# Placing weight tiles at chosen byte distances, modulo 256, from the other matmul operand

## The chip, the cores and the metric

One core of one Trainium2 chip runs the whole program. The metric is the device time of one execution in microseconds (us), as the median of several runs. A hardware profile of one execution stands beside it.

## The reference

One decoder layer on 256 tokens of width 2048, in float32: a half-step SwiGLU, a mixer of two branches, and a second half-step SwiGLU, each between two RMS norms.

```python
def swiglu(h, w_gate, w_up, w_down):
    return (jax.nn.silu(h @ w_gate) * (h @ w_up)) @ w_down
...
    h = rmsnorm(x, ffn1_norm_pre[l])
    x = x + MACARON_SCALE * rmsnorm(swiglu(h, ...), ffn1_norm_post[l])
    h = rmsnorm(x, mix_norm_pre[l])
    y = token_mixer(h, ...)   # sigmoid(gate_a)*attention + sigmoid(gate_b)*hgrn2, times w_out
    x = x + rmsnorm(y, mix_norm_post[l])
    h = rmsnorm(x, ffn2_norm_pre[l])
    x = x + MACARON_SCALE * rmsnorm(swiglu(h, ...), ffn2_norm_post[l])
```

Widths: the SwiGLU steps go from 2048 to 5632 and back; the mixer projects 2048 to 13376 columns, has 16 attention heads over latents of width 512, and 16 heads of a gated linear recurrence (hgrn2). Nearly all of the arithmetic is the products of 256 tokens with weight matrices.

## The kernel before

**Split operands.** Float32 precision is had from float32r matmuls by splitting each operand in two parts: `hi`, the value rounded to float32r, and `lo`, the remainder. A product is hi·hi + hi·lo + lo·hi. `load_w` brings 128x1024 weights (512 KB) by DMA into `raw`, ScalarE casts `raw` to `hi` (L101), VectorE subtracts to get `lo` (L102). The tiles `whi` and `wlo` have four buffers each of 1024 float32 a partition. Activations lie in tiles of the form [128, 2, K tiles, 256], whose second axis is hi and lo: `h` (the tiles h1, after1 and h2 in the program), `at`, `oa`, `ob`, `mg`, `cqT`, `ckvT`.

**Two kinds of product.** A TensorE matmul loads a stationary operand of 128 columns (LDWEIGHTS, the engine row PEld) and streams a moving operand past it. While one matmul streams, the stationary operand of the next is loaded.

- *Column products*, `gemm_t`: the weights are stationary and the activations move, so the outputs come out with the product's columns on the partitions. For each K tile and each half of 256 columns there is a pair: `lo` weights against 256 moving columns (L122, the activations' hi), and `hi` weights against 512 (L123, the activations' hi and lo side by side). For the first K tile the pair stands the other way round (L119, L120). One load of 1024 weights feeds eight such pairs. The gate and up products, all gates of the mixer, the q/f projections of hgrn2, both output projections of the branches and the small products of attention are of this kind: 4224 pairs.
- *Row products*, `gemm_n`: the activations are stationary and the weights move, 512 columns at a time, three matmuls for each K tile and half of the tokens (`_tok`: L138 hi·hi, L139 lo·hi, L140 hi·lo). One load feeds twelve matmuls. The down products, `w_out`, the first 512 columns of gate and up, the latents, the values and gates of hgrn2 and the rope part of the queries are of this kind; `w_v` too, with 256 columns at a time. At the end of a stage (`late`, `own`) some loads are held for a second pass; those lie in buffers `wpair` of the stage's pool, hi and lo one behind the other.

**Addresses.** A pool's tiles lie one behind the other in a partition. In the program before, all buffers of `whi` and `wlo` start at byte 96 modulo 256; `h`, `at`, `oa`, `ob`, `mg` and `wpair` at 224; `cqT` and `ckvT` at 160. Every K tile and half within a tile is a whole number of 256 bytes further on. So the distance, by which this document means *the start of the moving operand less the start of the stationary operand that is loaded meanwhile, modulo 256 bytes*, is one number for a whole product:

| product | moving, stationary | distance before |
|---|---|---|
| row, `whi`/`wlo` against `h`, `at`, `mg` | 96, 224 | 128 |
| row, `wpair` against `h`, `at`, `mg` | 224, 224 | 0 |
| row, `whi`/`wlo` against `cqT` (`q_rope`) | 96, 160 | 192 |
| row, 256 wide, against `ckvT` (`w_v`) | 96, 160 | 192 |
| column, `h`, `oa`, `ob` over `whi`/`wlo` | 224, 96 | 128 |
| column, `cqT`, `ckvT` over `whi`/`wlo` | 160, 96 | 64 |

**Order.** The program order of TensorE is that of the source: products follow each other without a break where their loads are early enough. All weight loads go out on one queue (SP), with four `raw` buffers ahead.

**Other tiles that the change touches.** `sg` in `ffn` holds a gate product of 256 columns from its end to the end of the up product after it (about 22 us), with two buffers; `z0`, `z1` are the tiles of the down product's results, unused until then. `rope_tables` has five small temporaries (`ang`, `turns`, three parts); `pT` holds transposed attention weights later on.

Of the kernel before, what the change touches and what calls it, by code (L numbers as in the profile page):

```python
# [9 lines left out]
F32 = mybir.dt.float32  # L10
# [33 lines left out]

WARM = 10

TWO_PI = 2.0 * np.pi
MAGIC = 1.5 * 2.0 ** 23

# [13 lines left out]
class Ops:  # L63


    def __init__(self, ctx, tc, a):
        self.tc, self.nc, self.a = tc, tc.nc, a
        self.const = ctx.enter_context(tc.tile_pool(name="const", bufs=1))
        self.wp = ctx.enter_context(tc.tile_pool(name="wp", bufs=1))
        self.small = ctx.enter_context(tc.tile_pool(name="small", bufs=3))  # L70
        self.hp = ctx.enter_context(tc.tile_pool(name="hp", bufs=1))
        self.mm = ctx.enter_context(tc.tile_pool(name="mm", bufs=2, space=PSUM))
        self.tp = ctx.enter_context(tc.tile_pool(name="tp", bufs=2, space=PSUM))
        self.sp = ctx.enter_context(tc.tile_pool(name="sp", bufs=2, space=PSUM))
        self.dram = ctx.enter_context(tc.tile_pool(name="dram", bufs=1, space=DRAM))
        self.slots = KF // 4
        self.mhalf = self.const.tile([P, 8], F32, name="mhalf")
        self.nc.vector.memset(self.mhalf, -0.5)
        self.ident = self.const.tile([P, P], F32, name="ident")


    def load_w(self, src, pool=None, pieces=1):
        nc = self.nc
        raw = self.wp.tile([P, 1024], F32, name="raw", bufs=4)
        if pieces > 1:
            hi = self.wp.tile([P, 1024], F32R, name="whi", bufs=4)
            lo = self.wp.tile([P, 1024], F32R, name="wlo", bufs=4)
            n = 1024 // pieces
            for i in range(pieces):
                c = slice(i * n, (i + 1) * n)  # L90
                nc.sync.dma_start(out=raw[:, c], in_=src[:, c])
                self.split(hi[:, c], lo[:, c], raw[:, c])
            return hi, lo
        nc.sync.dma_start(out=raw, in_=src)
        if pool is None:
            hi = self.wp.tile([P, 1024], F32R, name="whi", bufs=4)
            lo = self.wp.tile([P, 1024], F32R, name="wlo", bufs=4)
        else:
            both = pool.tile([P, 2, 1024], F32R, name="wpair", tag="s8", bufs=self.slots)
            hi, lo = both[:, 0], both[:, 1]  # L100
        nc.scalar.copy(out=hi, in_=raw)  # L101
        nc.vector.tensor_tensor(out=lo, in0=raw, in1=hi.bitcast(F32), op=ALU.subtract)  # L102
        return hi, lo

    def gemm_t(self, w, act, kt, tick=None):

        nc = self.nc
        ps = self.mm.tile([P, 2, 512], F32, name="mm")  # L110
        for g in range(kt // 4):
            hi, lo = self.load_w(w[g])
            for i in range(4):
                k = g * 4 + i
                for j in range(2):
                    c = slice(i * 256 + j * P, i * 256 + (j + 1) * P)
                    both = act(k)
                    if k == 0:
                        nc.tensor.matmul(ps[:, j], hi[:, c], both, start=True, stop=False)  # L119
                        nc.tensor.matmul(ps[:, j, 0:T], lo[:, c], both[:, 0], start=False, stop=False)  # L120
                    else:
                        nc.tensor.matmul(ps[:, j, 0:T], lo[:, c], both[:, 0], start=False, stop=False)  # L122
                        nc.tensor.matmul(ps[:, j], hi[:, c], both, start=False, stop=k == kt - 1)  # L123
            if tick:
                tick()
        return ps
# [12 lines left out]
        nc.tensor.matmul(o, both[:, 0, r], lo[:, c], start=False, stop=False)  # L139
        nc.tensor.matmul(o, both[:, 1, r], hi[:, c], start=False, stop=k == kt - 1)  # L140

    def gemm_n(self, w, act, kt, n=512, late=0, pool=None, own=0, hooks=(), tick=None):

        kg = 1024 // n
        banks = self.mm.tile([P, 2, 512], F32, name="mm")
        ps = [banks[:, 0], self.mm.tile([P, 2, 512], F32, name="mm")[:, 1] if late else banks[:, 1]]  # L150
        held = []
        hooks = list(hooks)

        def call(at):
            while hooks and hooks[0][0] <= at:
                hooks.pop(0)[1](ps)

        for g in range(kt // kg):
            hold = g * kg >= kt - late
            hi, lo = self.load_w(w[g], pool if hold and g * kg >= kt - late + own * kg else None)  # L160
            call(g * kg / kt - 1)
            for i in range(kg):
                k = g * kg + i
                self._tok(ps, hi, lo, act, k, kt, i, n, 0)
                if hold:
                    held.append((hi, lo, k, i))
                else:
                    self._tok(ps, hi, lo, act, k, kt, i, n, 1)
            if tick:
                tick()  # L170
        for m, (hi, lo, k, i) in enumerate(held):
            call(m / len(held))
            self._tok(ps, hi, lo, act, k, kt, i, n, 1)
        call(1)
        return ps if late else banks
# [128 lines left out]
def layer_kernel(ctx, tc, a, out):  # L304
# [75 lines left out]
    def ffn(n, act, fp, x_src, x_dst, nxt, hooks=(), fac=None, first=None):  # L380
        at = [fp.tile([P, 2, 4, T], F32R, name="at", tag="s8", bufs=ops.slots) for _ in range(KF // 4)]
        wg, wu = a[f"ffn{n}_w_gate"], a[f"ffn{n}_w_up"]


        if first:
            rows, first = first
        else:
            pg = ops.gemm_n(a[f"ffn{n}_w_gate0"], act, KD, late=KD, pool=fp, own=4, hooks=hooks)
            pu = ops.gemm_n(a[f"ffn{n}_w_up0"], act, KD, late=KD, pool=fp, own=4)
            rows = ops.rows(fac, fp.tile([P, T], F32, name="rows", tag="z0"))  # L390
            for tt in range(NT):
                sg = ops.small.tile([P, 512], F32, name="xn", bufs=2)
                S.activation(out=sg, in_=pg[tt], func=AF.Silu, scale=fac[:, tt, 2:3])
                V.scalar_tensor_tensor(out=sg, in0=pu[tt], scalar=fac[:, tt, 2:3], in1=sg, op0=ALU.mult, op1=ALU.mult)
                ops.transposed(sg, at[0], 0, tt)

        for c in range((FF - FF_N) // 256):
            pg = ops.gemm_t(wg[c], act, KD)
            if first and c == 0:
                for tt in range(NT):  # L400
                    ops.transposed(first[tt], at[0], 0, tt)
            sg = fp.tile([P, 2, T], F32, name="sg", bufs=2)
            ops.total(sg, pg, rows)
            S.activation(out=sg, in_=sg, func=AF.Silu)
            pu = ops.gemm_t(wu[c], act, KD)
            su = ops.small.tile([P, 2, T], F32, name="m", bufs=2)
            ops.total(su, pu, rows)
            V.tensor_tensor(out=sg, in0=sg, in1=su, op=ALU.mult)
            k = FF_N // P + 2 * c
            t, i = at[k // 4], k % 4  # L410
            ops.split(t[:, 0, i:i + 2], t[:, 1, i:i + 2], sg)
        new = operand(f"after{n}") if nxt else (None, None)
        fac = ops.factors(f"fac_after{n}") if nxt else None
        hooks = ops.closing(a[f"ffn{n}_w_down"], lambda k: at[k // 4][:, :, k % 4, :], KF, 16, 3, fp,
                    f"ffn{n}_norm_post", True, x_src, x_dst, (nxt, new[0], fac) if nxt else None)
        return *new, fac, hooks
# [69 lines left out]
def rope_tables(ops, pool):  # L486
# [7 lines left out]
    freq = pool.tile([P, HALF], F32, name="freq")  # L494
    nc.sync.dma_start(out=freq, in_=a["inv_freq"].broadcast_to([P, HALF]))
    n = NT * HALF
    ang = pool.tile([P, n], F32, name="ang")
    for tt in range(NT):
        V.tensor_scalar(out=ang[:, tt * HALF:(tt + 1) * HALF], in0=freq, scalar1=pos[:, tt:tt + 1],
                        scalar2=None, op0=ALU.mult)  # L500
# [2 lines left out]
        V.tensor_scalar(out=dst, in0=src, scalar1=MAGIC * step, scalar2=MAGIC * step, op0=ALU.add, op1=ALU.subtract)  # L503


    turns = pool.tile([P, n], F32, name="turns")
    parts = [pool.tile([P, n], F32, name=f"part{i}") for i in range(3)]
    for use in ((2, 1, 0), (0,)):
        V.tensor_scalar(out=turns, in0=ang, scalar1=1.0 / TWO_PI, scalar2=None, op0=ALU.mult)
        for i in use:  # L510
# [17 lines left out]
def mla(ops, mp, c_q, hm, h, fac, rows, oa, gate):  # L528
# [35 lines left out]

    hi, lo = ops.load_w(a["w_krope"][0])
    ps = ops.mm.tile([P, 2, 512], F32, name="mm")
    for k in range(KD):
        c = slice(k * ROPE, (k + 1) * ROPE)  # L570
# [23 lines left out]
    qrT = mp.tile([P, NH // 2, T], F32, name="qrT")  # L594

    def q_rope(c):
        ps = ops.gemm_n(a["w_q_rope"][c], cq, KL)
        for tt in range(NT):
            qr = small.tile([P, 8, ROPE], F32, name="xn", bufs=2)
            rope(qr, ps[:, tt].rearrange("p (a b) -> p a b", b=ROPE), tt, 8)  # L600
# [6 lines left out]
    def heads_in(pair, step):  # L607
        qn = mp.tile([P, 2, T], F32, name="qn", bufs=3)
        ops.total(qn, ops.gemm_t(a["w_q_nope"][pair], cq, KL))
        step()  # L610
        kn = mp.tile([P, 2, T], F32, name="kn", bufs=3)
        ops.total(kn, ops.gemm_t(a["w_k_nope"][pair], ckv, KL))
        step()
        ps = ops.gemm_n(a["w_v"][pair], ckv, KL, n=256)
        v = mp.tile([P, NT, 256], F32, name="v", bufs=3)
        S.copy(out=v, in_=ps[:, :, 0:256])
        return pair, qn, kn, v
# [389 lines left out]
```

## Time and profile before

| | |
|---|---|
| median of 3 runs | 2532.18 us (2531.83 to 2532.49) |
| the profiled execution's own time | 2530.82 us |
| its span, first to last instruction | 2528.9 us |
| mean granted TensorE clock | 0.999 |
| PE busy | 2512.3 us (99%) |
| PEld busy | 2144.2 us (85%) |
| VectorE, ScalarE, GpSimd busy | 1546.1 (61%), 1211.2 (48%), 82.1 us (3%) |
| moved by DMA | 482.12 MB, mean 191 GB/s |

Matmuls are pipelined, and a row's duration runs from a matmul's start to the modelled end of its results, which lies after the start of the next. The cost of one matmul in a dense stretch is therefore the step from its start to the next one's start, which the timeline shows to 10 ns; over many matmuls the mean step is known to a fraction of a nanosecond.

### The profile page before, as it was taken

To read this page: it belongs to the slowest core of one execution; us is meant where nothing else is said; L and a number is where in the kernel's file an instruction comes from. 1 tells how busy PE (TensorE), PEld (TensorE's weight loads), DVE (VectorE), ACT (ScalarE), POOL (GpSimd) and SP (SyncE) were. 2 spreads that over 40 slices of the span, in tenths; PEclk is the share of its full clock that TensorE was granted. 3 is DMA by queue.
4 is the path that set the end of the run, shared out by engine and by line. 5 is a ranking of instruction groups with operands and counts; after the bars stand their busy time and mean duration, and the time that the engine had idled before them with its cause. 6 is when DMAs were issued, how large, how long until landed. Compare 5 with 4: busy or idle time off the path is not lost.

```text
span 2528.9 us, 33917 instructions
## 1 busy us (share of the span) xinstructions
PE 2512.3 (99%) x13306; PEld 2144.2 (85%) x13306; DVE 1546.1 (61%) x1845; ACT 1211.2 (48%) x1605; POOL 82.1 (3%) x108
## 2 busy tenths in 40 slices
PE   9999999999999999999999999999999999999998
PEld 7888888888877898888888888888788888888887
DVE  5656656544466666558778876655655666654444
ACT  6444444444354566444555555445444444444433
POOL 0000000000000100000000001110000000000000
PEclk9999999999999999999999999999999999999999
DMA  8555555556575444555555555567655555555655
GB/s 299 185 188 187 185 190 189 186 191 201 194 282 181 162 135 149 189 184 183 175 166 168 167 166 175 191 223 235 221 188 188 186 188 187 185 190 191 196 196 183
DMA packets 137680, 482.12 MB, mean 191 GB/s; under 512 B 15920, under 2 KB 16432, under 8 KB 136752
## 3 DMA queue, kind: packets, MB, share of 16 engines
q1 hardware_dynamic: 137520, 479.96, 57.5%
q8 instruction: 104, 1.70, 0.3%
q14 instruction: 56, 0.46, 0.1%
HBM read 473.61 MB, written 6.29 MB: 190 GB/s over the span
## 4 chain that ended last, share of the span: by engine, by line
PE 97%; DVE 1%; DMA 1%; POOL 1%; issue 0%; ACT 0%; SPq 0%; DVEq 0%; POOLq 0%; ACTq 0%
PE mm L123 36%; PE mm L122 19%; PE mm L139 12%; PE mm L140 12%; PE mm L138 12%; PE mm L119 3%; PE mm L120 1%; PE sp L841 1%; PE sp L629 0%; PE sp L628 0%; PE sp L829 0%; PE tp L660 0%; DVE x L283 0%; PE tp L237 0%; DMA raw<-in_w_cq 0%
## 5 line engine op out<-in xcount | busy, mean ns | idle before, releaser
L102 DVE TENSOR_TENSOR wlo<-raw,whi 128x1024 fp32r<-128x1024 f32 x832 | 1031.5, 1242 | 701.9 <-ACT whi L101 695.1
L101 ACT CAST whi<-raw 128x1024 fp32r<-128x1024 f32 x832 | 872.7, 1050 | 866.1 <-PE mm L123 455.6
L123 PE MATMUL mm<-h,whi 128*128 128x512 f32 x2400 | 846.0, 393 | 0.0
L122 PE MATMUL mm<-h,wlo 128*128 128x256 f32 x2400 | 678.1, 283 | 0.0
L123 PEld LDWEIGHTS mm<-h,whi 128*128 128x128 f32 x2400 | 450.7, 188 | 100.7
L122 PEld LDWEIGHTS mm<-h,wlo 128*128 128x128 f32 x2400 | 451.2, 188 | 3.9
L123 PE MATMUL mm<-after,whi 128*128 128x512 f32 x960 | 339.5, 394 | 0.0
L122 PE MATMUL mm<-after,wlo 128*128 128x256 f32 x960 | 273.0, 284 | 0.0
L138 PE MATMUL mm<-whi,at 128*128 128x512 f32 x664 | 262.0, 395 | 0.0
L139 PE MATMUL mm<-wlo,at 128*128 128x512 f32 x664 | 262.0, 395 | 0.0
L140 PE MATMUL mm<-whi,at 128*128 128x512 f32 x664 | 261.7, 395 | 0.0
L123 PEld LDWEIGHTS mm<-after,whi 128*128 128x128 f32 x960 | 180.4, 188 | 39.3
L122 PEld LDWEIGHTS mm<-after,wlo 128*128 128x128 f32 x960 | 180.5, 188 | 1.5
L139 PEld LDWEIGHTS mm<-wlo,at 128*128 128x128 f32 x664 | 125.0, 188 | 29.4
L140 PEld LDWEIGHTS mm<-whi,at 128*128 128x128 f32 x664 | 125.1, 188 | 29.2
L138 PEld LDWEIGHTS mm<-whi,at 128*128 128x128 f32 x664 | 125.1, 188 | 29.1
L138 PE MATMUL mm<-whi,after 128*128 128x512 f32 x304 | 122.5, 403 | 0.4 <-ACT after L178 0.4
L140 PE MATMUL mm<-whi,after 128*128 128x512 f32 x304 | 120.1, 395 | 0.0
L139 PE MATMUL mm<-wlo,after 128*128 128x512 f32 x304 | 120.0, 395 | 0.0
L123 PE MATMUL mm<-oa,whi 128*128 128x512 f32 x240 | 84.6, 393 | 0.0
L123 PE MATMUL mm<-ob,whi 128*128 128x512 f32 x240 | 84.6, 393 | 0.0
L130 ACT COPY m<-mm 128x512 f32<-128x512 f32 x56 | 32.9, 588 | 97.1 <-PE mm L123 97.1
(306 smaller groups left out, 2819.4 us busy)
## 6 DMA issues: line engine op xcount, KB each, us to landing
raw<-in_ffn_w_down SPq DMA_DIRECT2D x176, 512.0 KB, 4.3
raw<-in_ffn_w_gate SPq DMA_DIRECT2D x175, 512.0 KB, 4.3
raw<-in_ffn_w_up SPq DMA_DIRECT2D x175, 512.0 KB, 4.3
raw<-in_w_ga SPq DMA_DIRECT2D x32, 512.0 KB, 3.4
raw<-in_mla_w_o SPq DMA_DIRECT2D x32, 512.0 KB, 3.8
raw<-in_w_hq SPq DMA_DIRECT2D x32, 512.0 KB, 3.5
raw<-in_w_hf SPq DMA_DIRECT2D x32, 512.0 KB, 3.4
raw<-in_w_hi SPq DMA_DIRECT2D x32, 512.0 KB, 3.5
```

The source lines that it names most:

```text
L101: nc.scalar.copy(out=hi, in_=raw)
L102: nc.vector.tensor_tensor(out=lo, in0=raw, in1=hi.bitcast(F32), op=ALU.subtract)
L119: nc.tensor.matmul(ps[:, j], hi[:, c], both, start=True, stop=False)
L120: nc.tensor.matmul(ps[:, j, 0:T], lo[:, c], both[:, 0], start=False, stop=False)
L122: nc.tensor.matmul(ps[:, j, 0:T], lo[:, c], both[:, 0], start=False, stop=False)
L123: nc.tensor.matmul(ps[:, j], hi[:, c], both, start=False, stop=k == kt - 1)
L130: self.nc.scalar.copy(out=out, in_=ps[:, :, T:512])
L138: nc.tensor.matmul(o, both[:, 0, r], hi[:, c], start=k == 0, stop=False)
L139: nc.tensor.matmul(o, both[:, 0, r], lo[:, c], start=False, stop=False)
L140: nc.tensor.matmul(o, both[:, 1, r], hi[:, c], start=False, stop=k == kt - 1)
L841: nc.tensor.matmul(ps[:, 0, j], B[:, j], A[:, j], start=True, stop=True)
```

## The change

The buffers of `whi` and `wlo` become 64 float32 (256 bytes) wider, and a part starts `place` float32 into its buffer. In row products the place is 32 (128 bytes), so `whi` and `wlo` start at 224 and the distance to `h`, `at`, `mg` is 0; 16 for `q_rope`, distance 0 to `cqT`; 0 for `w_v`, which keeps 192. In column products it goes round: with every load, `hi` moves by 8 float32 (32 bytes) through eight places, and with every eighth load `lo` does, so that 64 loads go through all 64 combinations. The small product with `w_krope` has place 0, as before. `wpair` is not touched. To make room (the wider buffers take 2048 bytes a partition), `sg` moves into the tag of `z1`, with one buffer in place of two, and the temporaries of `rope_tables` into a buffer of `pT`. The tiles that are added or taken away are whole numbers of 256 bytes, so no other tile's start changes modulo 256.

```diff
+SAME = 32
...
+    def part(self, name, place):
+
+        return self.wp.tile([P, 1024 + 64], F32R, name=name, bufs=4)[:, place:place + 1024]
+
-    def load_w(self, src, pool=None, pieces=1):
+    def load_w(self, src, pool=None, pieces=1, places=(SAME, SAME)):
...
-            hi = self.wp.tile([P, 1024], F32R, name="whi", bufs=4)
-            lo = self.wp.tile([P, 1024], F32R, name="wlo", bufs=4)
+            hi, lo = self.part("whi", places[0]), self.part("wlo", places[1])
...
+    def round(self):
+
+        i = self.count
+        self.count += 1
+        return i % 8 * 8, i // 8 % 8 * 8
+
     def gemm_t(self, w, act, kt, tick=None):
...
-            hi, lo = self.load_w(w[g])
+            hi, lo = self.load_w(w[g], places=self.round())
...
-    def gemm_n(self, w, act, kt, n=512, late=0, pool=None, own=0, hooks=(), tick=None):
+    def gemm_n(self, w, act, kt, n=512, late=0, pool=None, own=0, hooks=(), tick=None, place=SAME):
...
-            hi, lo = self.load_w(w[g], pool if hold and g * kg >= kt - late + own * kg else None)
+            hi, lo = self.load_w(w[g], pool if hold and g * kg >= kt - late + own * kg else None,
+                                 places=(place, place))
...
-            sg = fp.tile([P, 2, T], F32, name="sg", bufs=2)
+            sg = fp.tile([P, 2, T], F32, name="sg", tag="z1")
...
-    ang = pool.tile([P, n], F32, name="ang")
+    tmp = pool.tile([P, 3 * P], F32, name="angles", tag="pT", bufs=2)
+    ang, turns, *parts = (tmp[:, i * n:(i + 1) * n] for i in range(5))
...
-    turns = pool.tile([P, n], F32, name="turns")
-    parts = [pool.tile([P, n], F32, name=f"part{i}") for i in range(3)]
...
-    hi, lo = ops.load_w(a["w_krope"][0])
+    hi, lo = ops.load_w(a["w_krope"][0], places=(0, 0))
...
-        ps = ops.gemm_n(a["w_q_rope"][c], cq, KL)
+        ps = ops.gemm_n(a["w_q_rope"][c], cq, KL, place=SAME - 16)
...
-        ps = ops.gemm_n(a["w_v"][pair], ckv, KL, n=256)
+        ps = ops.gemm_n(a["w_v"][pair], ckv, KL, n=256, place=0)
```

More of the change, by code (lines that the diff above doesn't have):

```diff
@@ L76, in __init__ @@
         self.slots = KF // 4
+        self.count = 0
         self.mhalf = self.const.tile([P, 8], F32, name="mhalf")
@@ L95, in load_w @@
         if pool is None:
-            hi = self.wp.tile([P, 1024], F32R, name="whi", bufs=4)
-            lo = self.wp.tile([P, 1024], F32R, name="wlo", bufs=4)
+            hi, lo = self.part("whi", places[0]), self.part("wlo", places[1])
         else:
```

## The prediction, made before the change was run

> **What bounds the kernel now.** First the page's busy times, then its chain of waits: TensorE is busy nearly all the time, and the chain that ends last runs through it.
>
> ```profile
> PE 2512.3 (99%) x13306; PEld 2144.2 (85%) x13306; DVE 1546.1 (61%) x1845; ACT 1211.2 (48%) x1605; POOL 82.1 (3%) x108
> ```
>
> ```profile
> PE 97%; DVE 1%; DMA 1%; POOL 1%; issue 0%; ACT 0%; SPq 0%; DVEq 0%; POOLq 0%; ACTq 0%
> ```
>
> So time goes only if the steps from one matmul to the next shrink, and a step saved in a dense stretch is saved in the span. Next the groups by line, in which "x" is a count and the last number before the second bar a mean duration in ns:
>
> ```profile
> L102 DVE TENSOR_TENSOR wlo<-raw,whi 128x1024 fp32r<-128x1024 f32 x832 | 1031.5, 1242 | 701.9 <-ACT whi L101 695.1
> L101 ACT CAST whi<-raw 128x1024 fp32r<-128x1024 f32 x832 | 872.7, 1050 | 866.1 <-PE mm L123 455.6 <-PE mm L140 368.9 <-issue 16.8
> L123 PE MATMUL mm<-h,whi 128*128 128x512 f32 x2400 | 846.0, 393 | 0.0
> L122 PE MATMUL mm<-h,wlo 128*128 128x256 f32 x2400 | 678.1, 283 | 0.0
> ```
>
> L122 and L123 are the column products. For the row products the view of one line, L139, keeps the operands apart, with shortest, median and longest duration in ns:
>
> ```profile
> L139 PE MATMUL mm<-wlo,at x664: 387/393/404, 502.5 to 2513.5; 128*128 128x512 f32 x166
> L139 PE MATMUL mm<-wlo,after x304: 387/393/477, 750.0 to 1498.1; 128*128 128x512 f32 x152
> L139 PE MATMUL mm<-wlo,mg x108: 387/393/404, 1685.7 to 1767.1; 128*128 128x512 f32 x108
> L139 PE MATMUL mm<-wlo,h x96: 387/394/500, 6.4 to 1818.7; 128*128 128x512 f32 x96
> L139 PE MATMUL mm<-wlo,ckvT x64: 276/276/281, 834.1 to 975.3; 128*128 128x256 f32 x64
> L139 PE MATMUL mm<-wpair,at x40: 387/389/397, 729.8 to 2520.3; 128*128 128x512 f32 x40
> L139 PE MATMUL mm<-wpair,h x32: 389/389/505, 1788.0 to 1824.1; 128*128 128x512 f32 x32
> L139 PE MATMUL mm<-wpair,mg x20: 389/389/397, 1756.8 to 1776.4; 128*128 128x512 f32 x20
> L139 PE MATMUL mm<-wpair,after x16: 387/389/499, 755.5 to 775.2; 128*128 128x512 f32 x16
> L139 PE MATMUL mm<-wlo,cqT x16: 393/394/478, 820.9 to 853.1; 128*128 128x512 f32 x16
> ```
>
> The reader is to see that the median goes with the distance, whatever the operand: 393 or 394 at 128 (`wlo` against `at`, `after`, `mg`, `h`), 394 at 192 (`cqT`), 389 at 0 (all four `wpair` rows). At 128 there are 664 + 304 + 108 + 96 = 1172 on this line, and as many on L138 and L140, which run beside it: 3516 matmuls.
>
> Last the timeline, whose first column is each matmul's start. At the start of the second SwiGLU, `wpair` and `whi`/`wlo` take turns against the same `h`, each for 24 matmuls:
>
> ```profile
> 1808.09 0.39 PE L138 MATMUL mm<-wpair,h 128*128 128x512 f32 x1
> ...
> 1813.55 0.40 PE L138 MATMUL mm<-whi,h 128*128 128x512 f32 x1
> ...
> 1819.14 0.39 PE L138 MATMUL mm<-wpair,h 128*128 128x512 f32 x1
> ```
>
> At distance 0, 24 steps take 5.46 us, or 227.5 ns each; at 128, right behind, 5.59 us, or 232.9. Longer stretches, in the last down product, give the settled steps:
>
> ```profile
> 2470.02 0.40 PE L138 MATMUL mm<-whi,at 128*128 128x512 f32 x1
> ...
> 2512.78 0.39 PE L139 MATMUL mm<-wlo,at 128*128 128x512 f32 x1
> ...
> 2516.22 0.39 PE L139 MATMUL mm<-wpair,at 128*128 128x512 f32 x1
> ...
> 2520.30 0.39 PE L139 MATMUL mm<-wpair,at 128*128 128x512 f32 x1
> ```
>
> At 128, 184 steps in 42.76 us are 232.4 ns each; at 0, 18 steps in 4.08 us are 226.7. So a median duration of 389 goes with a step of 226.7, and durations stand some 162 ns above steps: 394 at 192 is a step of about 232, and 276, for `w_v` with 256 columns at 192, one of about 114.
>
> **The row products: a price that the trace shows.** 3516 matmuls go from 128 to 0. Settled, each saves 232.4 − 226.7 = 5.7 ns; in the runs of 24, 5.4. That is 3516 × 5.7 ns = 20.0 us, or 19.0. About 200 of them stand in the first stage, beside the loads of both forms of x; should that stage wait for its loads anyway, 1.1 us of it is not had. `q_rope`, from 192 to 0, has 48 matmuls at some 6 ns, 0.3 us; `w_v` stays. I take 20 us, between 18 and 21.
>
> **The column products: a price that must be bounded.** These are 4224 pairs, and going round puts them at distances that the trace mostly doesn't have. What it has:
>
> ```profile
> 859.14 0.40 PE L119 MATMUL mm<-ckvT,whi 128*128 128x512 f32 x1
> ...
> 859.50 0.28 PE L122 MATMUL mm<-ckvT,wlo 128*128 128x256 f32 x1
> ...
> 861.61 0.28 PE L138 MATMUL mm<-whi,ckvT 128*128 128x256 f32 x1
> ...
> 1961.66 0.28 PE L122 MATMUL mm<-h,wlo 128*128 128x256 f32 x1
> ...
> 1987.63 0.28 PE L122 MATMUL mm<-h,wlo 128*128 128x256 f32 x1
> ```
>
> With both parts at distance 128, 74 pairs take 25.97 us: 350.9 ns each. With both at 64, six pairs from 859.50 to 861.61 take 2.11 us, 351.7 ns. The pair from 859.14 to 859.50 is a dear one without a wait: 360 ns. The cheapest pair that rows allow to be put together is a 512-wide step as in the row products at 0 and a 256-wide one as in `w_v`: 226.7 + 114 = 340.7 ns. So the bounds are 4224 × (340.7 − 350.9) = −43 us and 4224 × (360 − 350.9) = +38 us.
>
> Between them I go by an average, since going round visits every distance equally often. Less 162, the groups' 283 and 393 are steps of 121 and 231, which make 352 against the pair's measured 350.9; I put them at 120.4 and 230.5. For the 512-wide step the row products give 226.7 at 0, 232.4 at 128 and 232 at 192, mean 230.4: no change. For the 256-wide one there is 120.4 at 128, about 121 at 64 (351.7 − 230.8), and 114 at 192: mean 118.5, or 1.9 ns less. If the quarter that no row shows, 0, is as good for 256 columns as it is for 512, the mean is 117.3, 3.1 ns less. I take 2.8, nearer to that, since 0 was the best of all distances in rows: 4224 × 2.8 ns = 12 us saved. That the distances of `hi` and `lo` act one by one, and that odd multiples of 32 bytes lie between their neighbours, is assumed; no row shows either.
>
> **The rest costs nothing, and why.** No instruction is added or removed. Casts and subtractions write at other places; should that be slower, its cover is large. Per load VectorE works 1.24 us and ScalarE 1.05 (L102, L101), while TensorE takes 8 × 351 ns = 2.81 us (columns) or 12 × 232 ns = 2.79 us (rows), and the casts wait for TensorE to free a buffer (their releasers), so the weights stand ahead; without that cover 1 ns on each of 832 casts would be 0.8 us. The one buffer of `sg` makes ScalarE's copy at the end of a gate product wait until the `sg` before has been read, and weight casts are queued behind that copy:
>
> ```profile
> L130 ACT COPY sg<-mm x40: 586/586/586, 63.5 to 2264.5; 128x512 f32<-128x512 f32 x40
> L404 ACT ACTIVATE sg<-sg x40: 632/633/639, 66.7 to 2266.5; 128x512 f32<-128x512 f32 x40
> L178 ACT CAST at<-sg x40: 621/622/628, 79.4 to 2279.5; 128x512 fp32r<-128x512 f32 x40
> ```
>
> The `sg` copied at 63.5 is cast last at 79.4 and subtracted right behind, by 81. The next copy is due 64 pairs × 351 ns = 22.5 us after the first, at 86. Some 5 us are left over, so nothing waits. `z1` is first written in the down product, and the temporaries of `rope_tables` are done with before attention writes `pT`. The weights are asked for 1.3% faster, which the cover above bears too.
>
> **Sum.** −20 − 12 = −32 us. The profiled execution took 2530.82 us, 1.9 more than its span and 1.4 less than the median of 2532.18; the median should come to 2500.
>
> A rule to set beside the rows: the Trainium skill, TensorE: Matmul & The Clock Gate, "Back-to-back issue gap", gives N/2.4 + 2.5 ns a matmul, 215.8 for 512 columns and 109.2 for 256. If placing took every step there, the estimate from that page is a saving of some 58 us in rows and 110 in columns; no stretch read above is that fast (226.7 and 114), so the trace does not bear it out.
>
> **Rivals.**
> *The columns pay back what the rows give (slower).* Going round breaks settled patterns: each load has a new distance of `hi`, every eighth a new one of `lo`, and a pair in disorder costs up to the 360 ns seen. It decides from 20 us / 4224 = 4.7 ns a pair, a mean of 355.6; with all pairs at 360 the sum is +38 − 20 = +18 us, 2550. For it: the 360 ns pair stands right behind a change of operand, and 512-wide steps are dear at both 128 and 192. Against: the six pairs that follow it are back at 351.7.
> *The columns lose a little,* 0 to 15 us: 2512 to 2527, most likely 2517.
> *All column stalls go:* pairs at 340.7, 43 us, 2469. Every distance would have to be as good as the best; the medians of 393 and 394 at two quarters speak against it.
> *The change does nothing:* `wpair` is faster for another reason, such as less splitting beside it in the held pass: 2532. Against: the runs of 24 follow each other in one gate product, and the step changes with each.
> The Trainium skill speaks for this rival: SBUF — State Buffer, "Who interferes with whom", has independent read ports for the moving operand and LDWEIGHTS, and says that "PE and ACT never wait on anyone". By that rule the sum is 0; the trace disagrees, with 227.5 against 232.9 ns at two distances.
>
> **How the numbers follow.** Changes within 0.2% (5 us) can't be told from none here. Chances: the forecast, with columns saving up to 40 us, 0.64; columns losing up to 15, 0.18; all stalls gone, 0.04; columns taking back all or more, 0.08; distance without effect, 0.06. Faster is the first three, 0.86; same is the last, 0.06; slower 0.08. The range leaves out the two cases at the top and the fastest one: from 2474 (rows 20, columns 38) to 2526 (rows 20 less 14).
>
> **What would show it.** Right: the last down product at 226 to 228 ns a step throughout; L139's medians at 389 for `at`, `after`, `mg`, `h` and `cqT` alike, with `wpair` and `w_v` as before; L122's mean falling from 283 towards 280, L123's staying near 393, each with more spread than before. Wrong: row steps still at 232 (distance is not the cause, or more address bits count), column pairs above 355 ns in the mean, or TensorE waiting for `whi` where it did not.

## The result, and the profile after

The changed kernel takes 2506.66 us (median of 4, 2506.02 to 2506.98) where the kernel before took 2532.01 beside it: a ratio of 0.9902 (95% interval 0.989 to 0.9914), or 25.3 us less. The forecast was 2500, 32 us less. Its profiled execution took 2506.64 us with a span of 2504.7. The page's busy times, and the columns' two costliest groups (L133 and L134 are L122 and L123 of before):

```profile
PE 2486.5 (99%) x13306; PEld 2136.1 (85%) x13306; DVE 1544.9 (62%) x1845; ACT 1210.7 (48%) x1605; POOL 82.2 (3%) x108
```

```profile
L134 PE MATMUL mm<-h,whi 128*128 128x512 f32 x2400 | 842.2, 394 | 0.0
L133 PE MATMUL mm<-h,wlo 128*128 128x256 f32 x2400 | 672.0, 280 | 0.0
```

The reader is to see the mean duration go from 283 down to 280 ns for the 256-wide matmul, and from 393 up to 394 for the 512-wide one. The view of L150 (L139 before) shows the row products, with shortest, median and longest duration:

```profile
L150 PE MATMUL mm<-wlo,at x664: 388/389/389, 500.0 to 2489.3; 128*128 128x512 f32 x166
L150 PE MATMUL mm<-wlo,after x304: 387/389/478, 741.8 to 1484.8; 128*128 128x512 f32 x152
L150 PE MATMUL mm<-wlo,mg x108: 389/389/397, 1671.6 to 1751.2; 128*128 128x512 f32 x108
L150 PE MATMUL mm<-wlo,h x96: 387/389/501, 6.8 to 1802.3; 128*128 128x512 f32 x96
L150 PE MATMUL mm<-wlo,ckvT x64: 276/280/284, 825.3 to 966.5; 128*128 128x256 f32 x64
...
L150 PE MATMUL mm<-wlo,cqT x16: 389/393/475, 812.0 to 844.1; 128*128 128x512 f32 x16
```

393 or 394 became 389 for `at`, `after`, `mg` and `h`, now at distance 0; `cqT`, at 0 too, shows 393. Against `at` the spread is gone: 388 to 389 over 664 matmuls, where before it was 387 to 404. The last down product's timeline agrees:

```profile
2446.00 0.39 PE L151 MATMUL mm<-whi,at 128*128 128x512 f32 x1
...
2488.84 0.39 PE L151 MATMUL mm<-whi,at 128*128 128x512 f32 x1
```

189 steps in 42.84 us are 226.7 ns. For the columns the best gauge is a whole stage: the gate and up products of the second SwiGLU are 40 products behind each other, and the view of the line that opens each product gives the first and the last start. Before (L119), then after (L130):

```profile
L119 PE MATMUL mm<-h,whi x80: 393/397/476, 1826.1 to 2264.6; 128*128 128x512 f32 x80
```

```profile
L130 PE MATMUL mm<-h,whi x80: 387/395/481, 1809.7 to 2246.3; 128*128 128x512 f32 x80
```

Between the two starts lie 39 products of 32 pairs and one pair, 1249 pairs: 438.5 us or 351.1 ns a pair before, 436.6 us or 349.6 after. Summed over all steps in the two traces, each from one matmul's start to the next one's, row products went from 934.4 to 916.1 us (−18.3), column products, `w_krope` among them, from 1498.4 to 1492.0 (−6.4), all else by +0.5: together the 24.2 us by which the span is shorter.

### The profile page after: what moved, and what is told of

Read it like the earlier page. It is cut to its first block, busy times and chain, and to the rows that moved or that the text cites. A ratio compares the mean times of both kernels' runs of the same rounds, so it can differ in the third digit from the quotient of the medians.

```text
span 2504.7 us, 33918 instructions
## 1 busy us (share of the span) xinstructions
PE 2486.5 (99%) x13306; PEld 2136.1 (85%) x13306; DVE 1544.9 (62%) x1845; ACT 1210.7 (48%) x1605; POOL 82.2 (3%) x108
## 4 chain that ended last, share of the span: by engine, by line
PE 97%; DVE 1%; POOL 1%; DMA 1%; issue 1%; ACT 0%; SPq 0%; DVEq 0%; POOLq 0%; ACTq 0%
PE mm L134 36%; PE mm L133 18%; PE mm L151 12%; PE mm L150 11%; PE mm L149 11%; PE mm L130 3%; PE mm L131 1%; PE sp L852 1%; PE sp L640 0%; PE sp L639 0%; DVE x L295 0%; PE sp L840 0%; PE tp L671 0%; DVE xn L263 0%; DVE wlo L107 0%
## 5 line engine op out<-in xcount | busy, mean ns | idle before, releaser
L134 PE MATMUL mm<-h,whi 128*128 128x512 f32 x2400 | 842.2, 394 | 0.0
L133 PE MATMUL mm<-h,wlo 128*128 128x256 f32 x2400 | 672.0, 280 | 0.0
L134 PEld LDWEIGHTS mm<-h,whi 128*128 128x128 f32 x2400 | 450.9, 188 | 101.1
L133 PEld LDWEIGHTS mm<-h,wlo 128*128 128x128 f32 x2400 | 451.2, 188 | 3.5
L134 PE MATMUL mm<-after,whi 128*128 128x512 f32 x960 | 337.8, 394 | 0.0
L133 PE MATMUL mm<-after,wlo 128*128 128x256 f32 x960 | 270.6, 282 | 0.0
L149 PE MATMUL mm<-whi,at 128*128 128x512 f32 x664 | 258.3, 389 | 0.0
L150 PE MATMUL mm<-wlo,at 128*128 128x512 f32 x664 | 258.3, 389 | 0.0
L151 PE MATMUL mm<-whi,at 128*128 128x512 f32 x664 | 258.0, 389 | 0.0
L134 PEld LDWEIGHTS mm<-after,whi 128*128 128x128 f32 x960 | 180.4, 188 | 39.3
L133 PEld LDWEIGHTS mm<-after,wlo 128*128 128x128 f32 x960 | 180.6, 188 | 1.5
L150 PEld LDWEIGHTS mm<-wlo,at 128*128 128x128 f32 x664 | 124.6, 188 | 26.0
L150 PE MATMUL mm<-wlo,after 128*128 128x512 f32 x304 | 118.5, 390 | 0.0
L134 PE MATMUL mm<-ob,whi 128*128 128x512 f32 x240 | 84.3, 394 | 0.0
L134 PE MATMUL mm<-oa,whi 128*128 128x512 f32 x240 | 84.1, 393 | 0.0
```

The lines of the kernel that those rows point to most:

```text
L149: nc.tensor.matmul(o, both[:, 0, r], hi[:, c], start=k == 0, stop=False)
```

## The experiments

Each run is named by its label. The theory at first: a matmul's step is set by the distance, rows and columns add up, and going round gives the columns a mean over distances. Against it stand that settled patterns matter and not distances, and that the weights' own place does it.

**One part alone.** `rows_only` keeps the columns at place 0, `round_only` the rows.

```diff
 rows_only
-            hi, lo = self.load_w(w[g], places=self.round())
+            hi, lo = self.load_w(w[g], places=(0, 0))
 round_only
-SAME = 32
+SAME = 0
...
+        ps = ops.gemm_n(a["w_q_rope"][c], cq, KL, place=0)
```

> Rows at distance 0 as in the change, columns left at (128, 128). Theory (the two parts add, each by its own distance): the sums of steps by product put 18.8 us of the 25.3 gained on the row products, so 2513 us, with column pairs at 351 ns as before. Rival (going round is worth more than the sums say, because rows also gain from columns before them): 2517 or more.

> Columns going round, rows at 128 as before. Theory: the columns' 6.4 us alone, 2525.5 us, row steps at 232.4 ns. Rival (what the columns gained came with the rows): 2532.

`rows_only` took 2513.42 us, `round_only` 2526.43, the kernel before 2531.44 beside them (ratios 0.9929, 0.9913 to 0.9946; and 0.998, 0.997 to 0.9989). So the gains are 18.0 and 5.0 us; the parts add up to within 2.3 us of the whole, and neither needs the other. The step sums say the same: `rows_only` has rows at 916.1 and columns at 1498.4 us, `round_only` 936.4 and 1492.1.

**Fixed distances for the columns.** The changed kernel's own trace holds runs of eight pairs of matmuls at each of the 64 pairs of distances. Their means lie between 343 and 355 ns, but for one: `hi` at 64 and `lo` at 0 had 340.0. `cols_64_0` holds it throughout (places 0 and 16 over the latents), `cols_96_64` holds a dear one, and `per_product` goes round with one pair of distances for each product.

```diff
 cols_64_0 (cols_96_64: (8, 16))
+    def gemm_t(self, w, act, kt, tick=None, places=(16, 32)):
...
+            hi, lo = self.load_w(w[g], places=places)
 per_product
+        places = self.round()
         for g in range(kt // 4):
-            hi, lo = self.load_w(w[g], places=self.round())
+            hi, lo = self.load_w(w[g], places=places)
```

> Rows as in the change, columns held at one pair of distances: 64 for hi, 0 for lo, the pair at which the 63 steps of it in the changed kernel's trace had a mean of 340.0 ns, against 349.9 over all 64 pairs of distances. Theory (the pair of distances sets the steps): all columns settle at 340 ns, 4224 x 9.9 ns = 42 us below the change, 2465 us. Rival (it is the going round that saves, by breaking a settled pattern, and any fixed pair settles near 351): about 2512, as with columns at (128, 128).

> As cols_64_0 with the columns held at (96, 64), one of the dearest pairs of distances in the run with one pair per product (354.3 ns a pair). Theory (a fixed pair of distances keeps its own step over the whole kernel): 354.3 against 341.5 in cols_64_0, 4096 x 12.8 ns = 52 us more, 2525 us; with rows at 128 too it would be slower than the kernel before. Rival (any fixed distances do, and cols_64_0 is fast since they do not change): 2473.

> Columns go round too, but with a new pair of distances for each product of 32 pairs of matmuls, not for each load of 8. Theory (going round gives the mean over settled pairs of distances): 2506 us, within 3 of the change. Rival (each change of distance costs some steps in disorder, and the change has 528 of them): 3 to 8 us less than the change, 2499 to 2503; it would show as a dearer first pair of matmuls of each load in the change.

`cols_64_0` took 2472.89 us against 2531.44: 0.9769 (0.9754 to 0.9783), 58.6 us less than the kernel before and 33.8 less than the change. It is the version that beats both. `cols_96_64` took 2521.43 against 2531.16 (0.9962, 0.9947 to 0.9977), `per_product` 2508.63 against 2531.44 (0.991, 0.9895 to 0.9924). The opening line of the stage in the second SwiGLU, for the three in this order:

```profile
L130 PE MATMUL mm<-h,whi x80: 390/397/476, 1787.6 to 2213.4; 128*128 128x512 f32 x80
```

```profile
L130 PE MATMUL mm<-h,whi x80: 393/396/481, 1819.5 to 2260.7; 128*128 128x512 f32 x80
```

```profile
L131 PE MATMUL mm<-h,whi x80: 389/394/478, 1810.7 to 2247.9; 128*128 128x512 f32 x80
```

Over 1249 pairs these are 340.9, 353.2 and 350.0 ns a pair, against 351.1 at (128, 128) and 349.6 going round. So the pair of distances does set the step, in both directions, and holding it does not bring the pattern of before back. `per_product` is 2 us slower than the change, not 3 to 8 faster: changing the distances 528 times costs nothing that can be seen in the time. In `cols_64_0` both steps fell, to the durations of the fastest row products (389 and 276):

```profile
L134 PE MATMUL mm<-h,whi 128*128 128x512 f32 x2400 | 820.5, 389 | 0.0
L133 PE MATMUL mm<-h,wlo 128*128 128x256 f32 x2400 | 663.2, 276 | 0.0
```

Yet it gained 34 us and not the 42 expected. One reason shows in its timeline. Two products in a row, at the same distances:

```profile
64.75 0.28 PE L133 MATMUL mm<-h,wlo 128*128 128x256 f32 x1
...
74.89 0.28 PE L133 MATMUL mm<-h,wlo 128*128 128x256 f32 x1
...
75.95 0.28 PE L133 MATMUL mm<-h,wlo 128*128 128x256 f32 x1
...
85.82 0.28 PE L133 MATMUL mm<-h,wlo 128*128 128x256 f32 x1
```

From 64.75 to 74.89 are 29 pairs of 349.7 ns, from 75.95 to 85.82 are 29 of 340.3. One pair of distances has more than one settled pattern, and a product keeps its pattern until something comes between; that what came before it decides which, is argued and not shown. 108 of the 128 large column products have a mean of 340 from their seventh to their 24th pair. The slow pattern is rare: it fills three products and part of a fourth, which hold 2.0 us over 340 ns a pair. The first three pairs of the other 124, such as 353, 341 and 353 ns, hold 4.9 us, and so do the small products over the latents; pairs broken by other matmuls hold another 2.0.

**Which side is moved.** `operands_128` is the kernel before, with unused bytes that move the operands and not the weights.

```diff
         self.slots = KF // 4
+        self.nc.vector.memset(self.small.tile([P, 32], F32, name="pad", bufs=1), 0.0)
```

> The kernel before with 128 unused bytes a partition between the weight buffers and all that comes behind them, so that the operands move by 128 and the weights stay at 96: rows (but for w_out) come to distance 0, columns to (0, 0). Theory (only the distance counts, whichever side is moved): rows about 17 us faster, columns at the 347.4 ns that the run with one pair of distances per product showed for (0, 0), against 351.2 there for (128, 128), 4096 x 3.8 ns = 16 us; in all 2499 us. Rival (the weights' own place counts, for instance beside raw or for the casts that write them): 2531.

It took 2519.76 us against 2531.16 (0.9955, 0.9938 to 0.9971). Its row products, in the view of their line (L140 here):

```profile
L140 PE MATMUL mm<-wlo,at x664: 387/389/392, 504.2 to 2502.5; 128*128 128x512 f32 x166
L140 PE MATMUL mm<-wlo,after x304: 387/389/478, 746.0 to 1490.9; 128*128 128x512 f32 x152
L140 PE MATMUL mm<-wlo,mg x108: 390/393/404, 1678.8 to 1760.4; 128*128 128x512 f32 x108
...
L140 PE MATMUL mm<-wpair,at x40: 389/389/397, 725.9 to 2509.3; 128*128 128x512 f32 x40
L140 PE MATMUL mm<-wpair,h x32: 389/389/496, 1781.1 to 1816.8; 128*128 128x512 f32 x32
L140 PE MATMUL mm<-wpair,mg x20: 390/393/404, 1749.9 to 1769.6; 128*128 128x512 f32 x20
```

With the weights where they were, 389 comes with the operand. The one operand that did not move, `mg`, keeps 393, and even `wpair`, always at 389 until now, shows 393 against it, since `wpair` moved and `mg` did not. So it is the distance, not either side's place. The columns missed what the theory gave: they should have fallen to 347.4 ns at (0, 0), but the opening line of the stage says otherwise:

```profile
L120 PE MATMUL mm<-h,whi x80: 389/395/476, 1818.8 to 2259.4; 128*128 128x512 f32 x80
```

440.6 us for 1249 pairs are 352.8 ns. Of its 128 large column products 113 settled near 353, in steps of 346/358/356 a pair. The other 15 came below: ten at 347, in patterns such as 345/348, and five, broken by other matmuls, between 348 and 351. All columns together took 5 us more than in the kernel before. `per_product` had held (0, 0) for two products and seen only the first kind. This is the second settled pattern again.

`cols_64_0_shift32` is `cols_64_0` with both sides moved by 32 bytes.

```diff
-        self.mhalf = self.const.tile([P, 8], F32, name="mhalf")
+        self.mhalf = self.const.tile([P, 16], F32, name="mhalf")[:, 0:8]
...
-            ps = self.gemm_n(w[c], act, kt)
+            ps = self.gemm_n(w[c], act, kt, place=place)
...
-                        x_mid[0], x_mid[1], ("ffn2_norm_pre", h2, fac))
+                        x_mid[0], x_mid[1], ("ffn2_norm_pre", h2, fac), SAME - 8)
```

> As cols_64_0, with everything but mg moved by 32 bytes (and the places for w_out mended), so all distances of the large products are the same, and operands and weights start at multiples of 64 bytes, where they stood at 32 beyond one. Theory (distance alone): 2473 us, row steps at 226.7 ns. Rival (a read that starts in the middle of a 64-byte block costs an extra step, and part of what is over the 216 ns for 512 columns is that): row steps against at below 222 ns while those against mg, which stay where they were, keep 226.7, and 2440 us or less.

2473.11 us against 2531.16 (0.9771, 0.9757 to 0.9786), the same as `cols_64_0`; row products stay at 389 against `at`, which moved, and `mg`, which did not:

```profile
L150 PE MATMUL mm<-wlo,at x664: 389/389/397, 490.2 to 2456.7; 128*128 128x512 f32 x166
...
L150 PE MATMUL mm<-wlo,mg x108: 389/389/398, 1650.0 to 1729.8; 128*128 128x512 f32 x108
```

Starting at a multiple of 64 bytes is worth nothing. The Trainium skill (TensorE: Matmul & The Clock Gate, "Back-to-back issue gap") has the formula N/2.4 + 2.5 ns for the gap of a single matmul on its own, 215.8 ns for 512 columns. No settled row step here came below 226.7, so for these products the measurement decides, and what lies between is not the start within 64 bytes. The bfloat16 matmuls that open the program, 512 wide and all with one stationary operand, do reach 216 ns, in the traces of the change and of `rows_sweep`.

**Other distances in the rows.** `rows_sweep` gives each row product a place of its own; `rows_round` lets the rows of `cols_64_0` go round, for all 64 pairs of distances of `whi` and `wlo`.

```diff
 rows_sweep (places of the passes: first down 40, 48, 56; last 8, 16, 24; w_out 33, 34, 36;
 w_hi 0, 4, 12, 20; w_hg 28, 30, 31, 44; w_v 0 to 56 in steps of 8)
-            ps = self.gemm_n(w[c], act, kt)
+            ps = self.gemm_n(w[c], act, kt, place=places[c])
 rows_round
-                                 places=(place, place))
+                                 places=self.round() if place == SAME else (place, place))
```

> The change with the row products at several distances, one for each product: the three plain passes of the first down product at 32, 64 and 96, of the last one at 160, 192 and 224, of w_out at 4, 8 and 16, w_hi and w_hg at 128, 144, 176, 208 and 240, 248, 252, 48, and w_v at all eight multiples of 32. Theory (the distance decides whether the two reads meet, in units of some width): settled steps of 226.7 ns for a band of distances about 0 and 232 to 234 elsewhere; the small shifts of 4, 8, 16 and of 240 to 252 show how wide the band is. Rival (0 is special only as the same address, modulo 256): everything but 0 at 232 or more. Time: 2518 us by the sum of either.

> cols_64_0 with the row products going round in place of the columns: each load of twelve matmuls has another pair of distances for whi and wlo, all 64 in turn (wpair and q_rope as they were). Theory (equal addresses modulo 256 are the one place where the two reads never meet in rows): no other pair of distances gives a step below 226.7 ns, the mean lies near the 232 to 234 of the settled stretches of rows_sweep, and the kernel takes 3000 x 6 ns = 18 us more than cols_64_0, 2491 us. Rival (226.7 is not the floor: some pair of unequal distances comes nearer to 216): a pair with steps below 222 ns, to be used for a faster version.

`rows_sweep` took 2521.80 us against 2531.16 (0.9964, 0.9948 to 0.9979), 4 more than expected. L150 in seven stretches of its two large down products, at distances 32, 64, 96, 160, 192, 224 and 0, one stretch a line:

```profile
L150 PE MATMUL mm<-wlo,at x72: 393/395/397, 504.7 to 554.4; 128*128 128x512 f32 x72
...
L150 PE MATMUL mm<-wlo,at x73: 392/392/396, 560.0 to 609.5; 128*128 128x512 f32 x73
...
L150 PE MATMUL mm<-wlo,at x72: 399/399/399, 624.6 to 674.3; 128*128 128x512 f32 x72
...
L150 PE MATMUL mm<-wlo,at x71: 392/397/400, 2270.2 to 2319.4; 128*128 128x512 f32 x71
...
L150 PE MATMUL mm<-wlo,at x72: 393/396/398, 2329.9 to 2379.6; 128*128 128x512 f32 x72
...
L150 PE MATMUL mm<-wlo,at x72: 392/395/396, 2390.1 to 2439.8; 128*128 128x512 f32 x72
...
L150 PE MATMUL mm<-wlo,at x44: 387/389/396, 2450.3 to 2479.6; 128*128 128x512 f32 x44
```

The mean step over whole passes was 233.3, 228.9, 233.4, 234.3, 233.3 and 233.3 ns in this order, and 227.0 at 0. In `w_out`, 4, 8 and 16 bytes gave 237.8, 232.8 and 231.7: four bytes above 0 is the dearest place of all that were tried. Below 0 it is otherwise. `w_hg` at 252, four bytes short of 0, stands in runs of 24 matmuls between those of the recurrence; here are its durations on L150 and nine steps of one run:

```profile
L150 PE MATMUL mm<-wlo,after x32: 387/388/395, 1370.4 to 1393.0; 128*128 128x512 f32 x32
```

```profile
1372.22 0.39 PE L149 MATMUL mm<-whi,after 128*128 128x512 f32 x1
...
1374.26 0.39 PE L149 MATMUL mm<-whi,after 128*128 128x512 f32 x1
```

These are 226.7 ns each, in the cycle of distance 0. Over its four runs, but for the first step of each, the mean is 228.3 ns; such runs at 0 in the changed kernel have 228.7. The other seven places of `w_hi` and `w_hg` lie between 230.0 (at 208) and 234.9 (at 240), with 232.1 at 248. So neither expectation came true as it stood: 0 is not the only place at 226.7, which speaks against the rival, and the band that the theory asked for holds, of the places tried, 252 and 0 alone. 64 gains part of it.

The eight products of `w_v`, 256 columns wide, visited the eight multiples of 32. The first was at 192, the third at 0:

```profile
L150 PE MATMUL mm<-wlo,ckvT x8: 276/276/279, 829.1 to 831.5; 128*128 128x256 f32 x8
...
L150 PE MATMUL mm<-wlo,ckvT x8: 279/283/283, 880.4 to 882.9; 128*128 128x256 f32 x8
```

Settled, they took 113.3 ns at 192, 120.0 at 0 and at 96, and 116.7 to 119.0 at the other five, 117.9 in the mean: for 256 columns 0 is among the dearest.

`rows_round` took 2489.59 us against 2530.98 (0.9837, 0.9808 to 0.9865), as expected. In the last three steps of a load's twelve, (0, 0) had a median of 226.7 ns and each of the other 63 pairs of distances 229.0 or more. Over all twelve steps (0, 0) is not the best: it takes about eight steps to settle and has 229.9, where `whi` at 128 with `wlo` at 0 has 228.8. In long products, where a step settles, no place tried for the rows beats the change's.

## Why the prediction came out as it did

**The bound** held: TensorE is busy for 99% before and after, and each step saved in a dense stretch came off the span.

**The rows** were forecast at 20 us and gave 18.3 by the step sums, 18.0 in `rows_only`. The 5.7 ns a matmul was right where products are long: against `at` 11.5 us over 1992 matmuls, 5.8 ns each. It was too much against `after`, 3.6 us over 912, 4.0 ns each: those products stand among the recurrence's matmuls, and at 0 the first ten steps or so behind each interruption lie between 224 and 236 ns before the cycle of 226.7 begins. At 128 the mean was 232.4 from the second step on; at 0 it is 228.7. The term that was mis-sized is "settled, each saves" for these 912, by 1.6 us. The expected 389 for `cqT` was 393: the first of its two products of 24 matmuls is broken up, and the second settles at 226.7 only after nine steps. And `w_v`, unmoved, rose from 276 to 280, since its last four products settled at 117.8 ns a step, where its first four, and all eight before, have 113.3; the view of L150 in two stretches shows it:

```profile
L150 PE MATMUL mm<-wlo,ckvT x32: 276/276/282, 825.3 to 891.9; 128*128 128x256 f32 x32
...
L150 PE MATMUL mm<-wlo,ckvT x32: 280/281/284, 913.6 to 966.5; 128*128 128x256 f32 x32
```

That is a second settled pattern at one distance once more. With 240 matmuls in all both are below 0.5 us.

**The columns** were forecast at 12 us and gave 6.4 in the step sums, 5.0 alone. The half for the 256-wide step nearly came true: against `h` it fell by 2.5 ns, from 120.3 to 117.7 (283 to 280 in durations), where 2.8 was taken. What failed is "mean 230.4: no change" for the 512-wide step; it rose by 1.0 ns, from 230.7 to 231.7 (393 to 394). That is 4 of the 5.6 us that are missing.

That mean rested on three distances, and on the assumption that odd multiples of 32 bytes lie between their neighbours. `rows_sweep` refutes it: 32 bytes took 233.3 ns, where 0 has 227.0 and 64 has 228.9. With 232.4 at 128, the rows' eight distances have a mean of 232.0, close to the 231.7 that going round gave. That 0 is as good for 256 columns as for 512 is refuted as well, by `w_v` at 120.0; that the mean of its eight distances, 117.9, still comes near what was taken is luck. With these two means the sum would have been 349.9 ns a pair against 350.9, 4 us saved: low by 2 us, where the forecast was high by 6.

The third assumption, that the distances of `hi` and `lo` act one by one, does not hold for a single pair: `lo` at 0 gives a 512-wide step of 226.2 ns with `hi` at 64 but 231.8 with `hi` at 0, from the third pair of a product on, in `per_product`. Two distances and the state in which a product is entered set the pair together. So the rows, once all eight distances are known, give about the mean of going round, but they could not tell which pair of distances is best.

**The rivals.** That columns pay back the rows is out for going round; what it rested on, disorder at each change of distance, does not show (`per_product`, 2 us slower without those changes). That all column stalls go was given 0.04 and set aside because "every distance would have to be as good as the best"; that is true of going round, and a single chosen pair reaches it: the 340.7 ns put together from two rows is what `cols_64_0` settles at. That distance does nothing is out by `operands_128`, and with it the rule that the Trainium skill has in SBUF — State Buffer, "Who interferes with whom", as far as it would make operands' places of no account: they changed a matmul's step by up to 11 ns (237.8 against 226.7).

**Nothing else** moved: VectorE and ScalarE are as busy as before to 2 us, and ScalarE's copies into `sg` wait for the end of their product as before (67.8 us in 40 waits, 68.9 before), none for an earlier reader of `sg`; the waits for `pT` are the same 4.9 us.

What stays open is the mechanism under the distances. That the read of the moving operand and the load of the next stationary one meet is argued from which distances count, not shown; and why 4 bytes above are worse than 128 and 4 bytes below as good as 0, and 64 better than 32, no run here tells.

## What to carry to other kernels

When TensorE is busy all the time and its steps are longer in one place than in another with the same shapes, compare the operands' addresses modulo 256 before looking for waits: here 128 bytes of padding, on either side, were worth 5 to 6 ns a matmul in long row products, and a chosen pair of places 10 ns a pair in column products; the same padding on the operands' side made the columns 5 us dearer. Distances that are not measured can't be put between their neighbours. An average over places hides the best one: lay out the step by pair of distances from one run that visits them all, take the lowest, and hold it. Then check it over whole products, since a pattern seen in runs of eight may be one of several.

## What the runs showed of the hardware

- Steps of float32r matmuls of equal shape lock into short cycles: 227, 227, 226 ns for rows at 0; pairs of 340 or 350 ns with `hi` at 64 and `lo` at 0, each pattern kept until other matmuls come between.
- No run went below 226.7 ns for the settled 512-column step of row products, 113.3 for the 256-column one, and 340.0 for both together in column products, where they split as 227 and 113 or 226 and 114. Single steps were shorter by up to 3 ns.
- Of the addresses, the distance modulo 256 was what counted in all that was tried: buffers 4096 and 4352 bytes apart, and both sides moved by 32 bytes, gave the same steps.
- In row products of 512 columns two distances reached 226.7 ns, 0 and 252; 4 gave 237.8.
